# The seam between attention and the gate units: when the operand sums, the loads and the first unit's products run

## The chip, the cores and the metric

The kernel runs on one core of a Trainium2 chip. Five engines work side by side, each on its own stream of instructions: TensorE (PE, matmuls into PSUM), VectorE (DVE), ScalarE (ACT), GpSimd (POOL) and SyncE (SP), which here only issues transfers between the core's memory SBUF and the device memory. An engine takes its instructions in order: one that waits holds up all behind it. The metric is the device time of one execution in microseconds (us), lower is better.

## The reference

One layer of a streaming encoder on x, 1024 tokens by 1024 features, in fp32:

```python
h = rmsnorm(x, norm_mix_g[li])
z = h @ w_in[li]
qa, fa, ia, ga, qb, kb, vb, gate_a, gate_b = jnp.split(z, split_at, axis=-1)
oa = hgrn2_mixer(qa, fa, ia, ga, lower_bounds[li], hgrn_onorm_g[li])
ob = band_attention(qb, kb, vb, attn_qnorm_g[li], attn_knorm_g[li], attn_rel_bias[li])
merged = (jax.nn.sigmoid(gate_a) * (oa @ w_branch_a[li])
          + jax.nn.sigmoid(gate_b) * (ob @ w_branch_b[li]))
x = x + merged @ w_out[li]
...
```

A feed-forward block and an embedding block follow, which the change does not touch. What matters here are gate_a and gate_b: 2048 output features, 16 columns of 128, each a product of the normalized x with a block of `w_in`, then a sigmoid.

## The kernel before

**Numbers.** Every fp32 matrix is split in two parts: `hi`, a rounded copy in the matmul's type that ACT casts, and `lo`, the remainder that DVE or POOL subtracts. A product is three matmuls (hi·hi, hi·lo, lo·hi) for each 128 x 128 block against 512 tokens. `self.u` holds the eight feature blocks of x, scaled and split: eight pairs of tiles of 128 x 1024, the halves `h0` and `h1` being 512 tokens each.

**Gate columns.** The first four of the 16 columns are plain products (`PLAIN = 4`): per column two token halves of eight blocks, 24 matmuls each. Columns 0 and 1 are computed by `gate`, which attention draws on as filler between its own steps; columns 2 and 3 in `gate_units`. The other twelve columns go through six *units* of Strassen's scheme in Winograd's form (`strassen`), two columns by two token halves each: seven products of 12 matmuls instead of eight. Its seven activation operands are listed in `self.sops`: 0, 4 and 6 are plain blocks of u (odd features h1, even features h1, even features h0); 1, 2 and 3 are sums of blocks (`t32`, `t1`); 5 is a further sum that is written over the odd features' h0 of u, by `mix_last`, when no plain product needs that any more. The weight operands of a unit come from `strassen_weights`: sums of quarters of a raw weight pair that `strassen_load` brings, each split in hi (ACT) and lo (DVE or POOL).

**The sums.** `mix_sums` takes four pairs k of feature blocks from x again: it loads two tiles, scales the odd one on ACT, makes the sums on DVE in place, casts on ACT, subtracts on DVE. Four steps a pair, with a `yield` between them, so that `gate_units` can deal them out between the pieces of its plain products.

**Order.** PE's matmuls, and all operations called through `self.V`, `self.A` and `self.G`, run on their engines in the order of the program text (`Pinned`); so do all transfers on SP's queue (`load` and `store`). Operations called through `self.nc` are placed by the compiler's scheduler; POOL's sums of other weights (`quad_slow`), which the units carry along, are of that kind. A tile's buffer comes free after the last use of the tile; `self.slot()` takes one of 32 buffers of 128 x 1024, `self.stmp()` one of eight of 128 x 512, and a load waits on SP's queue until its buffer is free.

**The seam.** `attention` runs 34 turns (`whole = 32`, and two more to end the pipeline); in each it draws two pieces from `feed`, and after the last turn it gives out what is left of `feed`, the second half of column 1. Then `gate_units` starts `mix_sums` (line 774), loads the first unit's raw weights, applies the sigmoids of columns 0 and 1, and computes columns 2 and 3 while the sums and the first unit's weights are made on the other engines; in the first piece the outputs of two attention heads and columns 0 and 1 are stored (lines 793 to 795). Lines 801 to 806 end the sums and write the last operand, line 814 loads the second unit's weights. Line 832 runs the units; while a unit's products run, its `side` makes the next unit's weights.

In `strassen` (line 1405) three banks of PSUM are used, with products 3, 4, 5 and 6 added on top of a bank that DVE or ACT has read before:

```python
product(1, b2, True)
u2 = add(tmp(), p1, b2)
...
product(3, b2, False)
```

Product 3 may start only when the add in front of it has read b2.

Of the kernel before, what the change touches and what calls it, by code (L numbers as in the profile page):

```python
# [17 lines left out]
P = 128  # L18
# [23 lines left out]
def f32(ap):  # L42
    return ap.bitcast(F32)
# [13 lines left out]
class Trunk:  # L57
# [581 lines left out]
    def attention(self):  # L639

        steps = [(2 * two + p, b) for two in range(2) for b in range(8) for p in range(2)]
        whole = len(steps)
        feed = chain(self.feed, self.gate(self.gates, ahead=3), self.gate(self.gates, ahead=2))
        sc, pts = {}, {}

        def stack(n):
            if n >= whole:
                return iter(())
            p, b = steps[n]
            if b == 0:  # L650
                for h in range(2):
                    bt = self.small(640, tag="bias")
                    self.load(bt, self.d["bias"][2 * p + h])
                    self.bias[p, h] = bt
            return self.attn_stack(p, b)

        def scores(n, h):
            stages = self.attn_scores(*steps[n], h)
            sc[n, h] = (*next(stages), stages)

        def stage(n, h):
            if 0 <= n < whole:
                next(sc[n, h][2], None)

        def pt(n, h):
            if 0 <= n < whole:
                pts[n, h] = self.attn_pt(*sc[n, h][:2])

        def pv(n):
            if 0 <= n < whole:  # L670
                self.attn_pv(*steps[n], (pts.pop((n, 0)), pts.pop((n, 1))), sc[n, 0][1])

        for i in range(FIRST, 8):
            next(feed, None)
            if i == FIRST:
                self.hgrn_gate()
            if i == 7:
                drain(stack(0))
                drain(self.hgrn_out())
        for n in range(whole + 2):  # L680
            stage(n - 1, 1)
            next(feed, None)
            if n < whole:
                if steps[n][1] == 0:
                    self.ob.append(self.slot())
                scores(n, 0)
# [12 lines left out]
            if n == 0:  # L699
                self.keep_heads(self.oa, self.od, self.done_heads)  # L700
            if n == whole // 2 + 3:
                self.keep_heads(self.ob, self.obd, [0, 1])
            yield 0
        yield from feed


    def gate(self, keep, ahead=AHEAD):
# [6 lines left out]
            self.nc.vector.tensor_tensor(t[:, hs], ps, self.rb[:, hs], ALU.mult)  # L714
            yield 1296

    def mix_sums(self):

        V, A = self.V, self.A
        h0, h1 = slice(0, HALF), slice(HALF, T)  # L720
        g = lambda c: self.cols[:, C_MIX + c:C_MIX + c + 1]
        self.t32, self.t1 = [], []
        xs = []

        def load(k):
            xs.append((self.slot(), self.slot() if k < 2 else self.fp.tile([P, D], F32, tag="raw", name=f"xo{k}")))
            for j in range(2):
                self.load(xs[k][j], self.d["x"][2 * k + j])

        load(0)  # L730
        load(1)
        for k in range(4):
            xe, xo = xs[k]
            A.activation(xo, xo, AF.Copy, scale=g(2 * k + 1))
            yield
            V.scalar_tensor_tensor(xo[:, h0], xe[:, h0], g(2 * k), xo[:, h0], ALU.mult, ALU.subtract)
            V.tensor_tensor(xo[:, h1], xo[:, h0], xo[:, h1], ALU.add)
            V.scalar_tensor_tensor(xe[:, h0], xe[:, h0], g(2 * k), xo[:, h1], ALU.mult, ALU.subtract)
            V.scalar_tensor_tensor(xe[:, h1], xe[:, h1], g(2 * k), xo[:, h1], ALU.mult, ALU.subtract)
            yield  # L740
            hi, lo = self.slot(F32R), self.slot(F32R)
            self.t32.append((hi, lo))
            A.copy(hi, xo)
            if k % 2 == 0:
                self.t1.append((self.slot(F32R), self.slot(F32R)))
            hi1, lo1 = [t[:, k % 2 * HALF:k % 2 * HALF + HALF] for t in self.t1[-1]]
            A.copy(hi1, xe[:, h0])
            yield
            V.tensor_tensor(lo, xo, f32(hi[:, :]), ALU.subtract)
            V.tensor_tensor(lo1, xe[:, h0], f32(hi1), ALU.subtract)  # L750
            if k < 2:
                load(k + 2)
            yield
        self.mix_last = [(self.u[2 * k + 1][0][:, h0], self.u[2 * k + 1][1][:, h0], xs[k][0][:, h1]) for k in range(4)]

    def gate_done(self, c, half, ps):
        hs = slice(half * HALF, half * HALF + HALF)
# [10 lines left out]
    def gate_units(self, sums):  # L768
# [2 lines left out]
        h0, h1 = slice(0, HALF), slice(HALF, T)  # L771
        self.gd = [self.spill() for _ in range(2 * KC)]
        self.kept = []
        side = self.mix_sums()
        next(side)
        self.strassen_load()
        weights = self.strassen_weights()
        ts, self.gates = self.gates, []
        for c, t in enumerate(ts):
            A.activation(t, t, AF.Sigmoid)  # L780
# [1 line left out]
        for c in range(2, PLAIN):  # L782
            (w,) = self.weights(1, ahead=PLAIN - 1 - c)
            for half in range(2):
                stream = self.feature(w, self.u, half, piece=2)
                while True:
                    try:
                        next(stream)
                    except StopIteration as e:
                        ps = e.value  # L790
                        break
                    next(side, None)
                    if c == 2 and half == 0 and self.kept:
                        self.keep_heads(self.ob, self.obd, [2, 3])
                        self.gate_keep()
                    next(side, None)
                    if c > 2 or half:
                        next(weights, None)
                self.gate_done(c, half, ps)
                next(side, None)  # L800
        drain(side)
        drain(weights)
        for hi, _, x in self.mix_last:
            A.copy(hi, x)
        for hi, lo, x in self.mix_last:
            V.tensor_tensor(lo, x, f32(hi), ALU.subtract)
        u, t = self.u, self.t32
        cut = lambda pair, h: [x[:, h] for x in pair]
        four = range(4)
# [1 line left out]
            [cut(u[2 * k + 1], h1) for k in four], [cut(t[k], h1) for k in four],  # L811
            [cut(self.t1[k // 2], slice(k % 2 * HALF, k % 2 * HALF + HALF)) for k in four], [cut(t[k], h0) for k in four],
            [cut(u[2 * k], h1) for k in four], [cut(u[2 * k + 1], h0) for k in four], [cut(u[2 * k], h0) for k in four]]
        self.strassen_load()
        units = (2 * KC - PLAIN) // 2
        for n in range(units):

            def side():
                more = self.strassen_weights() if n + 1 < units else self.branch_first()
                if n == 0:  # L820
                    yield
                    yield
                next(more, None)
                if n + 2 < units:
                    self.strassen_load()
                yield
                for _ in more:
                    if n + 1 < units:
                        next(sums, None)
                    yield  # L830

            self.strassen(lambda c, half, ps: self.gate_done(PLAIN + 2 * n + c, half, ps), side())
            yield 0
        self.gate_keep()

# [482 lines left out]

    def strassen_load(self):
        ap = self.sorder[self.snext]  # L1320
        pool = (self.rp, self.fp)[self.snext % 2]
        self.snext += 1
        raws = []
        for j in range(2):
            self.n += 1
            raw = pool.tile([P, D], F32, tag="raw", name=f"wr{self.n}")
            self.load(raw, ap[:, j * D:j * D + D])
            raws.append(raw)
        self.sraw.append(raws)
# [32 lines left out]
    def strassen_weights(self):  # L1362

        V, A, G = self.V, self.A, self.G
        r1, r2 = self.sraw.pop(0)
        h0, h1 = slice(0, HALF), slice(HALF, D)

# [37 lines left out]
    def strassen(self, done, side):  # L1405


        V = self.V
# [9 lines left out]
        def add(out, x, y):  # L1418
            V.tensor_tensor(out, y, x, ALU.add)
            return out  # L1420
# [2 lines left out]
        p1 = tmp()  # L1423
        self.A.copy(p1, b1)
        next(side, None)
        product(1, b2, True)
        u2 = add(tmp(), p1, b2)
        next(side, None)
        product(2, b3, True)
        next(side, None)  # L1430
        product(3, b2, False)
        u3 = add(tmp(), p1, b2)
        add(u3, u3, b3)
        done(1, 0, u3)
        next(side, None)
        product(4, b1, False)
        done(0, 1, b1)
        next(side, None)
        product(5, b2, False)
        done(1, 1, add(tmp(), p1, b2))  # L1440
        next(side, None)
        product(6, b3, False)
        done(0, 0, add(u2, u2, b3))
        drain(side)

    def keep_acts(self, k):
# [553 lines left out]
```

## Time and profile before

| | |
|---|---|
| Time, median of 3 runs (lowest to highest) | 1603.34 us (1603.18 to 1604.33) |
| Time of the profiled execution | 1603.3 us |
| Its span, first to last instruction | 1600.6 us |
| PE busy in the span | 1568.0 us (98%) |
| DVE, ACT, POOL busy | 1173.3, 643.7, 796.5 us |
| Mean granted clock of PE | 0.997 |
| Attention's last copy / unit 0's first product / unit 1's first product, from the span's start | 531.72 / 558.95 / 585.26 us |

How to read the lines: a row of the timeline has the start and the length in us, the engine, the line of the kernel (L54 and L83 are helpers that record every pinned operation), the operation, output<-inputs by the program's names, the shapes, and in brackets how long the engine stood idle before it and what ended that. `s` is a slot, `pm` a bank of PSUM, `xo` and `wr` raw tiles, `whi`/`wlo` a unit's weights, `q` a sum of weights, `t` a half tile of `stmp`, `m` a small tile, `d` device memory. PE's matmuls overlap, so a pair that is listed at 0.62 us is followed by the next group 0.46 us later.

### The profile page before, as it was taken

The page shows a single profiled execution, that of the slowest core. Times are in us where ns is not written, and L with a number is a line of the kernel's source. Part 1 is how long each engine was busy: PE and PEld are TensorE (multiplying, and loading weights), DVE is VectorE, ACT ScalarE, POOL GpSimd, SP SyncE. Part 2 cuts the span into 40 slices and gives each one's busy share as a digit, 9 for nine tenths or more (in the row PEclk, how much of TensorE's full clock was granted, in tenths as well). Part 3 has the DMA queues.
Part 4 walks back from the last instruction along what each step waited for, and adds up shares of the span by engine and source line. Part 5 has one row for each costly group of instructions (what it writes and reads, how often), then busy time and mean ns, then how long its engine had stood idle before and what let it go on. Part 6 is the DMA issues. An engine that isn't in the chain of part 4 may idle for free.

```text
span 1600.6 us, 21819 instructions
## 1 busy us (share of the span) xinstructions
PE 1568.0 (98%) x8224; PEld 1309.6 (82%) x8224; DVE 1173.3 (73%) x1759; ACT 643.7 (40%) x1085; POOL 796.5 (50%) x449
## 2 busy tenths in 40 slices
PE   8999999999999989999999999999999999999997
PEld 6998988878888868888888788888888888888886
DVE  5656665389898687545898988888888866764658
ACT  5321221177677433321376332222322233445553
POOL 3422221356653156324430777777777764644554
PEclk9999999999999999999999999999999999999999
DMA  5101000245762355375144433233333268885334
GB/s 190 53 28 46 35 28 27 99 153 188 227 217 107 112 204 187 140 295 220 66 145 171 159 105 99 99 99 99 102 110 103 84 251 320 306 282 193 125 133 157
DMA packets 81609, 230.52 MB, mean 144 GB/s; under 512 B 9184, under 2 KB 9952, under 8 KB 80992
## 3 DMA queue, kind: packets, MB, share of 16 engines
q1 hardware_dynamic: 81360, 229.12, 41.3%
q8 instruction: 64, 1.05, 0.3%
q14 instruction: 41, 0.34, 0.1%
q10 hardware_dynamic: 144, 0.02, 0.0%
HBM read 163.82 MB, written 65.27 MB: 143 GB/s over the span
## 4 chain that ended last, share of the span: by engine, by line
PE 81%; DVE 9%; POOL 2%; ACT 1%; issue 1%; DMA 1%; SPq 0%; POOLq 0%; DVEq 0%; ACTq 0%
PE pm L83 79%; DVE s L54 4%; DVE m L54 3%; PE pm L86 2%; DVE q L54 1%; POOL m L556 1%; ACT s L54 0%; DVE pm L54 0%; DMA d<-s 0%; DVE t L54 0%; ACT m L54 0%; DMA s<-in_oq 0%; POOL wl L126 0%; DVE wlo L54 0%; DMA wr<-in_fm 0%
## 5 line engine op out<-in xcount | busy, mean ns | idle before, releaser
L83 PE MATMUL pm<-s,wh 128*128 128x512 f32 (+1 forms) x1712 | 532.1, 392 | 5.6 <-ACT wh L123 5.4
L83 PE MATMUL pm<-s,whi 128*128 128x512 f32 x1568 | 489.6, 393 | 7.1 <-DVE t L54 7.0
L126 POOL TENSOR_TENSOR wl<-wr,wh 128x1024 fp32r<-128x1024 f32 (+2 forms) x108 | 269.7, 2502 | 389.8 <-ACT wh L123 386.5
L83 PEld LDWEIGHTS pm<-s,wh 128*128 128x128 f32 x1712 | 319.7, 189 | 72.9 <-ACT wh L123 5.9
L83 PEld LDWEIGHTS pm<-s,whi 128*128 128x128 f32 x1568 | 295.3, 189 | 74.0 <-DVE t L54 8.3
L83 PE MATMUL pm<-s,wl 128*128 128x512 f32 (+1 forms) x856 | 333.8, 390 | 0.5 <-POOL wl L126 0.5
L54 DVE TENSOR_TENSOR s<-s,s 128x512 f32<-128x512 f32 (+4 forms) x213 | 257.5, 1237 | 92.7 <-ACT s L54 55.2
L83 PE MATMUL pm<-s,wlo 128*128 128x512 f32 x784 | 308.3, 393 | 0.4 <-POOL wlo L54 0.4
L83 PE MATMUL pm<-wh,s 128*128 128x256 f32 (+1 forms) x896 | 238.2, 340 | 0.0
L123 ACT CAST wh<-wr 128x1024 fp32r<-128x1024 f32 (+2 forms) x114 | 115.0, 1009 | 263.8 <-PE pm L83 139.2
L83 PEld LDWEIGHTS pm<-s,wl 128*128 128x128 f32 x856 | 161.2, 188 | 34.7 <-POOL wl L126 1.5
L83 PEld LDWEIGHTS pm<-s,wlo 128*128 128x128 f32 x784 | 147.7, 188 | 34.5 <-POOL wlo L54 0.8
L83 PEld LDWEIGHTS pm<-wh,s 128*128 128x128 f32 x896 | 154.6, 190 | 13.9 <-DVE s L341 0.2
L54 DVE TENSOR_TENSOR t<-pm,t 128x512 f32<-128x512 f32 x136 | 93.4, 687 | 83.1 <-PE pm L83 79.8
L54 DVE TENSOR_TENSOR s<-pm,s 128x512 f32<-128x512 f32 (+1 forms) x134 | 87.4, 681 | 84.2 <-PE pm L83 83.9
L83 PE MATMUL pm<-wl,s 128*128 128x256 f32 (+1 forms) x448 | 147.5, 329 | 0.8 <-POOL wl L126 0.8
L54 POOL TENSOR_TENSOR wlo<-wr,whi 128x512 fp32r<-128x512 f32 (+1 forms) x55 | 111.2, 2030 | 64.5 <-DMA xo<-in_x 48.6
L54 ACT CAST whi<-q 128x512 fp32r<-128x512 f32 (+1 forms) x81 | 61.4, 758 | 157.2 <-DVE q L54 134.9
L54 POOL TENSOR_TENSOR s<-s,t 128x512 f32<-128x512 f32 x44 | 76.9, 1747 | 86.6 <-ACT t L54 86.6
L54 ACT CAST s<-s 128x1024 fp32r<-128x1024 f32 (+1 forms) x94 | 90.2, 980 | 67.4 <-DVE s L54 33.5
L54 POOL TENSOR_TENSOR wlo<-q,whi 128x512 fp32r<-128x512 f32 x54 | 90.5, 1676 | 53.0 <-ACT whi L54 39.2
L83 PEld LDWEIGHTS pm<-wl,s 128*128 128x128 f32 x448 | 85.4, 191 | 6.3 <-POOL wl L126 1.0
(148 smaller groups left out, 1953.0 us busy)
## 6 DMA issues: line engine op xcount, KB each, us to landing
d<-s SPq DMA_DIRECT2D x147, 256.0 KB, 3.4
s<-d SPq DMA_DIRECT2D x67, 512.0 KB, 6.0
wr<-d SPq DMA_DIRECT2D x36, 512.0 KB, 3.9
s<-in_wq SPq DMA_DIRECT2D x22, 512.0 KB, 6.1
wr<-in_sg SPq DMA_DIRECT2D x22, 512.0 KB, 4.1
wr<-in_su SPq DMA_DIRECT2D x22, 512.0 KB, 4.0
s<-in_x SPq DMA_DIRECT2D x21, 512.0 KB, 7.7
d<-s SPq DMA_DIRECT2D x18, 512.0 KB, 4.1
```

What stands on the lines that cost most here:

```text
L54: return lambda *a, **k: self.trunk.order(op(*a, **k), self.key)
L83: return self.order(self.nc.tensor.matmul(*a, **k))
L86: return self.order(self.nc.tensor.transpose(*a, **k))
L123: self.nc.scalar.copy(hi[:, c], raw[:, c])
L126: rest.tensor_tensor(lo[:, c], raw[:, c], f32(hi[:, c]), ALU.subtract)
L556: nc.gpsimd.tensor_tensor(ss, ss, self.mhalf[:, 0:8], ALU.pow)
```

## The change

Four things move.

1. *The sums of pairs 0 and 1 start in attention.* In turn 30 attention loads the first unit's raw weights and then the four tiles of pairs 0 and 1 (`mix_start`); in turns 32 and 33, between the pieces of `feed` that are left and after them it makes their sums, to the end.
2. *Loads ahead of stores.* `gate_units` begins with the loads of pairs 2 and 3 (their odd tiles now in two half tiles of `stmp` each) and of the second unit's raw weights; the stores follow as before.
3. *The first unit's weights come ahead of the sums of pairs 2 and 3*, and all their remainders are subtracted by DVE, none by POOL (`strassen_weights(V)`). The last operand is written during the last half of column 3 (`mix_last`, now a generator).
4. *Unit 0 runs its products in the order 0, 4, 6, 1, 2, 3, 5* (`early`), each of 4, 5 and 6 in a bank of its own, which DVE adds up: six banks instead of three, and two adds more. The other units are as before.

```diff
@@ attention @@
+            if n == whole - 2:
+                self.strassen_load()
+                self.mix_start()
+                tail = chain(self.mix_sums(0), self.mix_sums(1))
+            if n >= whole:
+                next(tail)
             yield 0
-        yield from feed
+        for x in feed:
+            next(tail, None)
+            yield x
+        drain(tail)
...
+    def mix_start(self):
+
+        self.t32, self.t1, self.xs = [], [], []
+        for k in range(2):
+            xe, xo = self.slot(), self.slot()
+            self.mix_load(k, xe, [xo[:, :HALF], xo[:, HALF:]], xo)
+
+    def mix_load(self, k, xe, xo, whole=None):
+        self.xs.append((xe, xo, whole))
+        self.load(xe, self.d["x"][2 * k])
+        if whole is not None:
+            self.load(whole, self.d["x"][2 * k + 1])
+        else:
+            for j in range(2):
+                self.load(xo[j], self.d["x"][2 * k + 1][:, j * HALF:j * HALF + HALF])
...
@@ mix_sums(self, k): one pair, the same operations in five steps @@
+        for x, _ in parts:
+            A.activation(x, x, AF.Copy, scale=g(2 * k + 1))
+        yield
+        V.scalar_tensor_tensor(x0, xe[:, h0], g(2 * k), x0, ALU.mult, ALU.subtract)
+        V.tensor_tensor(x1, x0, x1, ALU.add)
+        yield
+        for x, c in parts:
+            A.copy(hi[:, c], x)
+        V.scalar_tensor_tensor(xe[:, h0], xe[:, h0], g(2 * k), x1, ALU.mult, ALU.subtract)
+        V.scalar_tensor_tensor(xe[:, h1], xe[:, h1], g(2 * k), x1, ALU.mult, ALU.subtract)
+        yield
+        A.copy(hi1, xe[:, h0])
+        for x, c in parts:
+            V.tensor_tensor(lo[:, c], x, f32(hi[:, c]), ALU.subtract)
+        yield
+        V.tensor_tensor(lo1, xe[:, h0], f32(hi1), ALU.subtract)
+        yield
...
@@ gate_units @@
-        side = self.mix_sums()
-        next(side)
+        for k in (2, 3):
+            self.mix_load(k, self.slot(), [self.stmp(), self.stmp()])
         self.strassen_load()
-        weights = self.strassen_weights()
+        side = chain(self.strassen_weights(V), self.mix_sums(2), self.mix_sums(3))
...
+                if c == PLAIN - 1 and half:
+                    drain(side)
+                    side = self.mix_last()
...
-                    if c > 2 or half:
-                        next(weights, None)
...
-        drain(weights)
-        for hi, _, x in self.mix_last:
-            A.copy(hi, x)
-        for hi, lo, x in self.mix_last:
-            V.tensor_tensor(lo, x, f32(hi), ALU.subtract)
...
-        self.strassen_load()
...
-            self.strassen(lambda c, half, ps: self.gate_done(PLAIN + 2 * n + c, half, ps), side())
+            self.strassen(lambda c, half, ps: self.gate_done(PLAIN + 2 * n + c, half, ps), side(), early=n == 0)
...
@@ strassen_weights @@
-        V, A, G = self.V, self.A, self.G
+        V, A, G = self.V, self.A, engine or self.G
...
@@ strassen @@
+        if early:
+            b4, b5 = self.mm(), self.mm()
+            product(4, b4, True)
+            done(0, 1, add(tmp(), p1, b4))
+            next(side, None)
+            product(6, b5, True)
+            next(side, None)
         product(1, b2, True)
         u2 = add(tmp(), p1, b2)
+        if early:
+            add(u2, u2, b5)
         next(side, None)
         product(2, b3, True)
         next(side, None)
         product(3, b2, False)
         u3 = add(tmp(), p1, b2)
-        add(u3, u3, b3)
-        done(1, 0, u3)
+        done(1, 0, add(tmp() if early else u3, u3, b3))
         next(side, None)
-        product(4, b1, False)
-        done(0, 1, b1)
+        if early:
+            done(0, 0, add(u2, u2, b3))
+        else:
+            product(4, b1, False)
+            done(0, 1, b1)
+            next(side, None)
+        if early:
+            b6 = self.mm()
+            product(5, b6, True)
+            done(1, 1, add(u3, u3, b6))
+        else:
+            product(5, b2, False)
+            done(1, 1, add(tmp(), p1, b2))
         next(side, None)
-        product(5, b2, False)
-        done(1, 1, add(tmp(), p1, b2))
-        next(side, None)
-        product(6, b3, False)
-        done(0, 0, add(u2, u2, b3))
+        if not early:
+            product(6, b3, False)
+            done(0, 0, add(u2, u2, b3))
         drain(side)
```

More of the change, by code (lines that the diff above doesn't have):

```diff
@@ L715, in gate, with mix_sums @@
             yield 1296
-    def mix_sums(self):
+    def mix_start(self):
[11 more added lines that the diff above has]
+                self.load(xo[j], self.d["x"][2 * k + 1][:, j * HALF:j * HALF + HALF])
+    def mix_sums(self, k):
         V, A = self.V, self.A
@@ L721, in mix_sums @@
         g = lambda c: self.cols[:, C_MIX + c:C_MIX + c + 1]
[L722 to L731, printed above, removed]
-        for k in range(4):
[L733 to L753, printed above, removed]
@@ L754, in mix_sums @@
-        self.mix_last = [(self.u[2 * k + 1][0][:, h0], self.u[2 * k + 1][1][:, h0], xs[k][0][:, h1]) for k in range(4)]
+        xe, (x0, x1), xo = self.xs[k]
+        hi, lo = self.slot(F32R), self.slot(F32R)
+        self.t32.append((hi, lo))
+        if k % 2 == 0:
+            self.t1.append((self.slot(F32R), self.slot(F32R)))
+        hi1, lo1 = [t[:, k % 2 * HALF:k % 2 * HALF + HALF] for t in self.t1[-1]]
+        parts = [(xo, slice(0, T))] if xo is not None else [(x0, h0), (x1, h1)]
+        for x, _ in parts:
+            A.activation(x, x, AF.Copy, scale=g(2 * k + 1))
@@ L756, in gate_done, with mix_last @@
+        yield
+        V.tensor_tensor(lo1, xe[:, h0], f32(hi1), ALU.subtract)
+        yield
+    def mix_last(self):
+        h0, h1 = slice(0, HALF), slice(HALF, T)
+        for k in range(4):
+            self.A.copy(self.u[2 * k + 1][0][:, h0], self.xs[k][0][:, h1])
+        yield
+        for k in range(4):
+            hi, lo = self.u[2 * k + 1]
+            self.V.tensor_tensor(lo[:, h0], self.xs[k][0][:, h1], f32(hi[:, h0]), ALU.subtract)
+            if k % 2:
+                yield
     def gate_done(self, c, half, ps):
@@ L1320, in strassen_load @@
         ap = self.sorder[self.snext]
-        pool = (self.rp, self.fp)[self.snext % 2]
+        pool = self.fp if self.snext % 2 else self.rp
         self.snext += 1
@@ L1360, in unit_up, with strassen_weights @@
         self.V.tensor_tensor(self.gu[c][:, hs], ps, self.gu[c][:, hs], ALU.mult)
-    def strassen_weights(self):
-        V, A, G = self.V, self.A, self.G
+    def strassen_weights(self, engine=None):
+        V, A, G = self.V, self.A, engine or self.G
         r1, r2 = self.sraw.pop(0)
@@ L1403, in strassen_weights, with strassen @@
         self.sready = (a11, cut(s21, h0), cut(s21, h1), s3, cut(a12, h0), cut(a12, h1), s4)
-    def strassen(self, done, side):
+    def strassen(self, done, side, early=False):
         V = self.V
```

## The prediction

> **What bounds the kernel now.** I read the busy shares first, then the waits of TensorE by stage, then the stretch around the seam in windows and in order of time.
>
> ```profile
> PE 1568.0 (98%) x8224; PEld 1309.6 (82%) x8224; DVE 1173.3 (73%) x1759; ACT 643.7 (40%) x1085; POOL 796.5 (50%) x449
> ```
>
> PE is busy for 1568.0 of 1600.6 us, so no change that leaves the matmuls alone can win more than its 32.6 idle us and what the clock loses. The windows cut the seam at PE's own steps: unit 0 of the Strassen units, the hole in it, the stretch after the hole, unit 1 up to its own small hole, and the following 19.11 us, in which seven products run without a gap.
>
> ```profile
> 515.00:531.60 16.60, 16.60 (x133) 13.39 (x130) 7.80 (x25) 6.61 (x14) 0.00 (x0) 1.00 0.08 33
> 558.95:585.26 26.31, 21.30 (x85) 16.71 (x84) 18.78 (x24) 11.06 (x19) 8.41 (x6) 0.94 0.48 170
> 567.80:572.69 4.89, 0.00 (x1) 0.00 (x1) 3.23 (x5) 3.62 (x8) 1.27 (x1) 0.98 0.74 215
> 572.69:576.33 3.64, 3.64 (x10) 2.87 (x10) 1.47 (x2) 0.62 (x1) 1.28 (x1) 0.56 1.00 351
> 585.26:594.55 9.29, 8.42 (x38) 6.58 (x36) 8.99 (x7) 3.45 (x7) 9.21 (x6) 1.00 0.81 270
> 594.55:613.66 19.11, 19.11 (x83) 15.66 (x84) 15.13 (x15) 7.73 (x12) 16.05 (x11) 1.00 0.75 254
> ```
>
> (Columns: length, then busy us of PE, PE's weight loads, DVE, ACT, POOL; granted clock, DMA share, GB/s.) Unit 0 takes 26.31 us where seven undisturbed products take 19.11, or 2.73 each: 7.20 us are lost. 4.89 is the hole. After it the clock is 0.56 for 3.64 us, which loses 3.64 x 0.44 = 1.60. In PE's order of time:
>
> ```profile
> 563.81 1.01 PE L83 MATMUL pm<-s,whi 128*128 128x512 f32 x2
> ...
> 564.89 0.63 PE L83 MATMUL pm<-s,whi 128*128 128x512 f32 x2
> ...
> 572.69 1.22 PE L83 MATMUL pm<-s,whi 128*128 128x512 f32 x2 [4.89 <-DVE t L54]
> ...
> 594.55 0.72 PE L83 MATMUL pm<-s,whi 128*128 128x512 f32 x2 [0.87 <-DVE t L54]
> ```
>
> The hole is product 3 waiting for the add that frees bank b2 (tile t). A smaller one, 0.87, stands at product 3 of unit 1. The pair at 563.81 is 0.38 longer than the pair at 564.89. The chain shows what made the add late:
>
> ```profile
> 564.19 1.77 DVE s L54
> ...
> 568.87 0.52 ACT s L54
> ...
> 569.41 1.07 DVE s L54 x2
> ...
> 571.36 0.68 DVE s L54
> 572.03 0.61 DVE t L54
> ```
>
> In front of the add, in DVE's fixed order, stand the four remainders of the operand that is written last (569.41 to 572.03), and they wait for ACT's casts. DVE and ACT are behind; the sums' arithmetic starts only when attention has ended. DVE had room earlier: 7.80 busy of 16.60 us from 515.00 to 531.60.
>
> **The change part by part.** PE's 84 matmuls a unit stay: nothing is removed there.
>
> *Sums of pairs 0 and 1 begin in turns 32 and 33.* Durations on DVE and on the engines it meets:
>
> ```profile
> 527.55 0.48 ACT L54 COPY m<-pm 128x384 f32<-128x384 f32 x1 [0.26 <-PE pm L86]
> ...
> 531.72 0.27 ACT L54 COPY s<-pm 128x128 f32<-128x128 f32 x1 [3.69 <-PE pm L83]
> ...
> 531.88 1.16 ACT L54 ACTIVATE s<-s,cols 128x1024 f32<-128x1024 f32 x1
> ...
> 533.07 0.75 DVE L54 SCALAR_TENSOR_TENSOR s<-s,cols,s 128x512 f32<-128x512 f32 x1 [1.91 <-ACT s L54]
> ...
> 537.38 0.69 DVE L714 TENSOR_TENSOR s<-pm,rb 128x512 f32<-128x512 f32 x1 [3.56 <-PE pm L83]
> ...
> 538.71 1.41 DVE L54 SCALAR_TENSOR_TENSOR s<-s,cols,s 128x512 f32<-128x512 f32 x2
> ...
> 569.41 2.62 DVE L54 TENSOR_TENSOR s<-s,s 128x512 fp32r<-128x512 f32 x4 [1.65 <-ACT s L54]
> ```
>
> ```profile
> L54 DVE TENSOR_TENSOR wlo<-q,whi 128x1024 fp32r<-128x1024 f32 x1 | 1.2, 1215 | 0.0
> ```
>
> The scaling of pair 0 (1.16) goes behind ACT's copy at 527.55, so 528.0 to 529.2, in 3.69 us in which ACT waited; DVE starts at 529.2 instead of 533.07. A pair costs DVE 0.75 + 0.69 + 1.41 + 1.22 + 0.69 = 4.76. In the tail nothing of attention stands behind these but the copy at 531.72, on which no matmul of the gates depends. Cost on PE: nothing. Without that cover it would be the 1.16 of one scaling.
>
> *The first unit's weight remainders go from POOL to DVE, pairs 2 and 3 behind them.*
>
> ```profile
> 547.79 1.36 POOL L54 TENSOR_TENSOR wlo<-wr,whi 128x512 fp32r<-128x512 f32 x1 [48.58 <-DMA xo<-in_x]
> ...
> 548.03 1.67 DVE L54 TENSOR_TENSOR xo<-xo 128x512 f32<-128x512 f32 x1
> ...
> 555.69 2.77 POOL L54 TENSOR_TENSOR wlo<-wr,whi 128x1024 fp32r<-128x1024 f32 x1 [6.54 <-ACT whi L54]
> ...
> 556.25 3.43 DVE L54 SCALAR_TENSOR_TENSOR s<-s,cols,xo 128x512 f32<-128x512 f32 x2
> ```
>
> DVE gets 3 x 0.69 + 1.22 = 3.3 us more, but beside POOL's operations its own were stretched: 1.67 for 0.69, 3.43 for 1.41, 1.77 (at 564.19) for 0.69, together 4.1. So the move is about even; I count +3.3 and let the 4.1 go, since undisturbed durations are used throughout. [...]
>
> DVE's ledger up to unit 0: four pairs 19.0, weights 4 x 0.69 + 1.22 = 4.0, moved remainders 3.3, last operand 2.6, five gate products 3.4: 32.3 us, from 529.2 to 561.5 without a wait. Waits for ACT were 1.91 and 1.65 above; two to four of them make it 565 to 568. The pairs themselves end some 4 us before that (2.6 and two gate products come after them).
>
> *Unit 0's order becomes 0, 4, 6, 1, 2, 3, 5.* Products 4 and 6 use plain blocks. From 558.95 at 2.73 each, product 1 needs the sums at 567.14 instead of 561.68; product 3 needs b2 free at 572.60 instead of 567.14; product 5, the only reader of the last operand, starts at 575.33. Ahead of the add u2 DVE has one more add and multiply (1.4), so it reaches it at 566.4 to 569.4, and product 1 ends at 569.87: in time by 2 us or more. The two more adds of unit 0 (0.69 each) are that one and one behind u2 that frees nothing PE waits for. If the early start brought nothing at all, the order alone would do most: add end 572.64 + 1.4 + 3.3 - 4.1 = 573.2 against 572.60, a hole of 0.6.
>
> *SP's order.*
>
> ```profile
> 488.04 2.25 SPq L78 DMA_DIRECT2D s<-in_x  x4
> ...
> 492.50 7.07 SPq L78 DMA_DIRECT2D wr<-in_sz  x2
> ...
> 527.32 12.20 SPq L78 DMA_DIRECT2D d<-s  x4
> ...
> 540.04 0.72 SPq L78 DMA_DIRECT2D xo<-in_x  x1
> ...
> 568.27 1.83 SPq L78 DMA_DIRECT2D wr<-in_sz  x4
> ...
> 574.65 0.78 DVE L54 TENSOR_TENSOR q<-wr,wr 128x512 f32<-128x512 f32 x1 [2.01 <-DMA wr<-in_sz]
> ```
>
> ```profile
> s<-in_x SPq DMA_DIRECT2D x21, 512.0 KB, 7.7
> ```
>
> The first four x loads now come behind the sz pair: 499.6 to 501.9, landed by 509.6, used at 528.0. They need four of the 32 slots; in turn 30 27 are held (16 of u, 2 of v, 6 of the keys, 2 of ob, 1 gate). If none came free before attention's last copy at 531.72, they would land near 540, DVE's ledger would start 11 us later and the hole would be back at 6 to 10 us. The count excludes it, and so does 488.04: the same four loads found slots long before attention ended. The x loads of pairs 2 and 3 (six, four of them halves) and unit 1's sz pair pass the four stores of 527.32. Their tiles lie where attention's were, so between 531.6 and the end of the tail near 540: landed by 548 at the latest, needed near 548; each late us eats one of the 5 us that the pairs have before 567.14. The stores behind them still wait for ACT's sigmoids (about 541 with the tail ahead), as the ones before did. The 2.01 us wait at 574.65 goes.
>
> *Sum.* 4.89 + 1.60 + 0.38 = 6.87. The hole of 0.87 in unit 1 I leave standing. The profiled execution took 1603.3 (span 1600.6 and 2.7 around it), as the median of the runs, 1603.34. 1603.3 - 6.9 = **1596.4**.
>
> **What is late next: unit 1.**
>
> ```profile
> 580.51 1.29 POOL L1046 TENSOR_TENSOR s<-s,s 128x512 f32<-128x512 f32 x1 [5.63 <-DVE q L54]
> ...
> 587.08 2.85 POOL L54 TENSOR_TENSOR wlo<-wr,whi 128x1024 fp32r<-128x1024 f32 x1
> ...
> 587.59 2.89 DVE L54 TENSOR_TENSOR q<-wr,q 128x512 f32<-128x512 f32 x1
> ...
> 589.90 3.45 POOL L54 TENSOR_TENSOR wlo<-q,whi 128x512 fp32r<-128x512 f32 x2
> ```
>
> POOL's remainder for product 3 ends near 591.6; PE wanted it at 593.45 (585.26 + 3 x 2.73). Now PE wants it at 578.06 + 8.19 = 586.25. If POOL's quad sums, whose place is not written by hand, start as late as now, that is a wait of 5.4 and with a new clock loss 7.0; if unit 1's remainders go first, as their raw weights now lie there early, nothing. I take nothing, being nearest to the POOL time free before 580.51 (5.63 us).
>
> **The rivals.**
> - *Unit 1 takes part of it back* (POOL late, or DVE stretched beside it as at 587.59). 1 to 7 us; I price it by the middle, 3.4: **1599.8**. For: POOL is 9.21 of 9.29 busy there. Against: the unit's weights start without the 2.01 wait. [...]
> - *The early start brings nothing* (x late, or ACT holds the tail): the hole of 0.6 remains: **1597.0**.
> - *Slower: DVE stays the bound through units 0 and 1.* Then its 3.3 of remainders and 1.4 of adds only lengthen its queue: the add at 593.8 that ends the 0.87 hole comes 4.7 later, at 598.5, and product 3 of unit 1 with it: 1603.3 + 4.7 = **1608.0**. It needs DVE to have no idle time to fill and the stretching to stay; against it stand its 8.8 idle us before 531.60 and the waits of 3.56, 2.01, 1.91 and 1.65.
>
> **How the numbers follow.** Forecast 0.62, early start without use 0.10, unit 1 0.20, slower 0.08. Low end: the 0.87 and the unnamed 0.3 of unit 0 go too, 1595.2, with 0.5 for the measurement: 1594.7. High end: 1601.5, inside rival 1, which leaves out its upper third, the slower case and little else. About 0.2% or 3.2 us can be told from no change, so faster means below 1600.1: 0.62 + 0.10 + over half of 0.20, and 0.79 after a little for what I overlook; within 0.13; slower 0.08.
>
> **What would show it.** Right: unit 0 takes 19 to 20 us at clock 1.00, no PE idle at product 3, x loads issued near 500, the raw weights of unit 1 before the stores, DVE busier from 528 to 533. Wrong: PE waits on DVE s at product 1, on POOL wlo or DVE t in unit 1, or a clock below 1.00 before 600.

## The result, and the profile after

| | before | after |
| --- | --- | --- |
| median of the runs compared, us | 1603.84 (1603.18 to 1604.98, 4 runs) | **1595.4** (1594.02 to 1597.2, 4 runs) |
| ratio, with its 95% interval | | 0.9947 [0.993, 0.9965] |
| the profiled execution, time and span, us | 1603.3, 1600.6 | 1595.63, 1593.7 |

The change made the kernel 8.4 us faster; the forecast was 1596.4. The interval lies wholly below 1.

Busy time of each engine on the page of the kernel after:

```profile
PE 1566.2 (98%) x8224; PEld 1309.3 (82%) x8224; DVE 1171.8 (74%) x1767; ACT 643.7 (40%) x1089; POOL 783.6 (49%) x445
```

The work has not shrunk: PE has as many matmuls and 1.8 us less busy time (the 3.41 us at clock 0.50, from 572.46 to 575.87 before, are gone), and DVE has 1172 us as before, in eight more instructions. So the gain is in when things happen. The windows after are cut at attention's last turns, then unit 0 and unit 1, each from its first matmul to the next unit's first (columns as in the prediction's windows):

```profile
515.00:531.60 16.60, 16.60 (x135) 13.40 (x131) 9.59 (x28) 7.65 (x15) 0.00 (x0) 1.00 0.18 64
559.08:578.46 19.38, 19.38 (x85) 15.79 (x84) 12.50 (x18) 7.28 (x12) 7.19 (x5) 1.00 0.45 150
578.46:597.80 19.34, 19.34 (x86) 15.80 (x84) 15.94 (x17) 7.91 (x13) 17.69 (x11) 1.00 0.79 243
```

Unit 0 takes 19.38 us where it took 26.31, at clock 1.00, and PE is busy in all of it. Unit 1 has no hole either and takes 19.34 us, so a product takes 2.76 us there (19.34 / 7). In the first row DVE is busy 9.59 of 16.60 us instead of 7.80: that is the arithmetic of the sums that has moved into attention's last turns. The chain of waits, cut to this stretch, says the same in one line:

```profile
527.81 112.28 PE pm L83 x503
```

From 527.81 on, through the plain columns and the first Strassen units, the chain is PE itself for 112 us; nothing releases it. DVE's timeline shows how much room there now is:

```profile
529.25 0.75 DVE L54 SCALAR_TENSOR_TENSOR s<-s,cols,s 128x512 f32<-128x512 f32 x1 [0.91 <-ACT s L54]
...
558.34 0.69 DVE L54 TENSOR_TENSOR s<-s,s 128x512 fp32r<-128x512 f32 x1
...
560.84 2.50 DVE L54 TENSOR_TENSOR s<-s,s 128x512 fp32r<-128x512 f32 x4 [1.21 <-ACT s L54]
...
566.44 0.69 DVE L54 TENSOR_TENSOR q<-wr,wr 128x512 f32<-128x512 f32 x1
567.16 0.69 DVE L54 TENSOR_TENSOR q<-q,wr 128x512 f32<-128x512 f32 x1
570.38 1.42 DVE L54 TENSOR_TENSOR t<-pm,t 128x512 f32<-128x512 f32 x2 [2.53 <-PE pm L83]
...
584.53 0.68 DVE L54 TENSOR_TENSOR t<-pm,t 128x512 f32<-128x512 f32 x1
```

The last row of pair 3 is the one at 558.34, so the pairs end at 559.0, just when unit 0 starts. The add u2, which PE waited 4.89 us for before, is the first of the two at 570.38, and now DVE waits 2.53 us for PE there: the wait has changed sides. DVE was through with everything in front of it at 567.85. PE wants bank b2 with the first matmul of product 3, the 61st of the unit:

```profile
572.91 0.64 PE L83 MATMUL pm<-s,whi 128*128 128x512 f32 x2
```

An add of 0.7 begun at 567.85 would have ended at 568.55, so DVE has 572.91 - 568.55 = **4.4 us of room**. Unit 1's add u2 (584.53) ends at 585.2, 1.5 us ahead of its product 3, which starts at 586.73.

SP's queue, issue time and how long the issue took:

```profile
499.77 2.10 SPq L78 DMA_DIRECT2D s<-in_x  x4
...
527.15 0.33 SPq L78 DMA_DIRECT2D s<-in_x  x1
...
533.22 0.85 SPq L78 DMA_DIRECT2D wr<-in_sz  x2
534.17 7.47 SPq L78 DMA_DIRECT2D d<-s  x4
```

The four x loads of pairs 0 and 1 go out from 499.77 on, within 2.10 us. The fifth, the first of pair 2, waits 25.3 us for PE to be done with a tile and goes out at 527.15; nothing behind it minds. Unit 1's raw weights (533.22) are ahead of the stores.

### The profile page after: what moved, and what is told of

It is laid out like the page before. It is cut to its first block, busy times and chain, and to the rows that moved or that the text cites. A ratio compares the mean times of both kernels' runs of the same rounds, so it can differ in the third digit from the quotient of the medians.

```text
span 1593.7 us, 21834 instructions
## 1 busy us (share of the span) xinstructions
PE 1566.2 (98%) x8224; PEld 1309.3 (82%) x8224; DVE 1171.8 (74%) x1767; ACT 643.7 (40%) x1089; POOL 783.6 (49%) x445
## 3 DMA queue, kind: packets, MB, share of 16 engines
q8 instruction: 64, 1.05, 0.2%
## 4 chain that ended last, share of the span: by engine, by line
PE 80%; DVE 9%; POOL 2%; ACT 2%; issue 2%; DMA 1%; SPq 0%; POOLq 0%; ACTq 0%; DVEq 0%
PE pm L83 77%; DVE s L54 5%; PE pm L86 2%; DVE m L54 2%; ACT s L54 1%; POOL wl L126 1%; POOL m L556 1%; DVE q L54 0%; DVE wl L126 0%; ACT wh L123 0%; DVE pm L54 0%; DMA d<-s 0%; DMA s<-in_oq 0%; POOL s L1075 0%; DMA wr<-d 0%
## 5 line engine op out<-in xcount | busy, mean ns | idle before, releaser
L126 POOL TENSOR_TENSOR wl<-wr,wh 128x1024 fp32r<-128x1024 f32 (+2 forms) x108 | 265.0, 2460 | 395.9 <-ACT wh L123 392.6
L54 POOL TENSOR_TENSOR wlo<-wr,whi 128x512 fp32r<-128x512 f32 (+1 forms) x53 | 107.5, 2037 | 74.9 <-ACT whi L54 74.1
```

The source lines that it names most:

```text
L54: return lambda *a, **k: self.trunk.order(op(*a, **k), self.key)
L126: rest.tensor_tensor(lo[:, c], raw[:, c], f32(hi[:, c]), ALU.subtract)
```

## The experiments

The theory: DVE was too late for the first unit because the sums' arithmetic began only after attention, and beginning it in attention's last turns is what removes the hole. The rivals: the new product order alone does it; moving the loads ahead of the stores does it; or taking the weights' remainders off POOL does it. Eleven kernels ran in three groups, each group beside runs of the kernel before on the same chip (medians 1604.02, 1603.85 and 1603.62). The table puts PE's waits in units 0 and 1 in the profiled execution together with an estimate of what the clock lost after them (PE's busy time at a granted clock of 0.50, times 0.5), and beside it the difference of the medians.

| | PE's waits in units 0 and 1 | clock | sum | median against before, us |
| --- | --- | --- | --- | --- |
| before | 4.89 + 0.87 | 1.60 | 7.4 | |
| after, taken again | 0 | 0 | 0 | -7.6 |
| order of products as before | 0 | 0 | 0 | -9.3 |
| order of products alone | 3.65 + 0.63 + 0.55 | 1.43 | 6.3 | +0.4 |
| no early start | 3.01 + 1.06 | 1.60 | 5.7 | -2.1 |
| loads behind the stores | 0 | 0 | 0 | -10.9 |
| remainders left on POOL | 0 | 0 | 0 | -6.1 |
| 2.4 us more on DVE | 0.57 | 0 | 0.6 | -7.8 |
| 9.8 us more on DVE | 4.97 + 0.60 | 2.54 | 8.1 | +0.2 |
| early start alone | 0.23 + 3.81 + 0.43 | 1.71 | 6.2 | -1.6 |
| early start and weights first | 0 | 0 | 0 | -7.8 |
| early start and loads first | 0.51 | 0 | 0.5 | -7.0 |

Two groups stand apart: with no long hole 6 to 11 us are won, with one 0 to 2. Within the first group the medians differ by more than the seam does (single runs of one kernel lie 3 to 7.5 us apart), so nothing is ranked there.

**Order of the products as before** (the rest of the change kept):

```diff
-            self.strassen(..., side(), early=n == 0)
+            self.strassen(..., side(), early=False)
```

> Unit 0 keeps its old order 0 to 6; early start, loads and weights first stay. If the early start of the sums carries the gain, nothing is lost: pair 3's remainder ends at 559.0 and product 1 would want it at 561.8, the add u2 can run at 565.1 and product 3 wants its bank at 567.3, so no hole, 1595.4 within 1. If the new order carries it, PE waits 3 to 5 us on DVE in unit 0: 1598.5 to 1602.

1594.74 (1593.39 to 1597.87), ratio 0.9937 [0.9912, 0.9961], and no PE wait between 545 and 615. Unit 0 starts at 561.28 in this execution, and in the old order its product 3, which wants b2, at 569.55. DVE's timeline:

```profile
567.31 0.69 DVE L54 TENSOR_TENSOR t<-pm,t 128x512 f32<-128x512 f32 x1 [1.18 <-ACT t L54]
```

In the old order u2 is the add at 567.31 and ends at 568.0, 1.5 us ahead. So with the sums begun early the new order is only spare room.

**Order of the products alone** (the kernel before, with the changed function and `early` for its first unit):

```diff
-            self.strassen(..., side())
+            self.strassen(..., side(), early=n == 0)
```

> The kernel before with the new order of unit 0 alone. The prediction's reckoning (order alone does most) would leave a hole of 0.6 at product 3 and 1597.0. Against it: product 6 now comes third, at 564.4, and wants the weights s4, which POOL ended at 569.7 in the kernel before: a hole of 5.3 there, with the clock's loss 5 to 7, so 1601 to 1604, nothing won.

1604.43 (1602.12 to 1605.19), ratio 0.9998 [0.9988, 1.0007]: nothing won. PE and ACT in order of time:

```profile
568.43 0.72 PE L83 MATMUL pm<-s,whi 128*128 128x512 f32 x2 [3.65 <-ACT whi L54]
...
569.78 0.80 PE L83 MATMUL pm<-s,wlo 128*128 128x512 f32 x1 [0.63 <-POOL wlo L54]
```

```profile
567.24 0.63 ACT L54 ACTIVATE t<-t 128x512 f32<-128x512 f32 x1 [3.14 <-DVE t L54]
567.77 0.60 ACT L54 CAST whi<-q 128x512 fp32r<-128x512 f32 x1
```

The hole moves to the third product, number 6, whose weight sum comes last in the kernel before. Its cast (567.77) stands on ACT behind a sigmoid that waits 3.14 us for DVE. DVE's lateness reaches PE by another way; reordering PE's demands does not help while the supply is late.

**No early start** (the change without beginning pairs 0 and 1 in turns 32 and 33; their x is still loaded in turn 30, weights first on DVE, loads first, new order):

```diff
-                tail = chain(self.mix_sums(0), self.mix_sums(1))
-            if n >= whole:
-                next(tail)
...
-        side = chain(self.strassen_weights(V), self.mix_sums(2), self.mix_sums(3))
+        side = chain(self.strassen_weights(V), *map(self.mix_sums, range(4)))
```

> The changed kernel without the early start: x of pairs 0 and 1 is still loaded in turn 30, but their sums are made in the gate units, behind the first unit's weights. By the prediction's reckoning a hole of 0.6, 1597.0. By the ledger as the trace of the changed kernel has it, DVE comes to the add u2 some 8 us later than 567.9: a hole of 3 to 4.5 at product 3, 1599 to 1601.

1601.88 (1599.82 to 1605.27), ratio 0.9989 [0.9978, 1.0]. PE's rows with a wait, then DVE's timeline:

```profile
578.95 1.22 PE L83 MATMUL pm<-s,whi 128*128 128x512 f32 x2 [3.01 <-DVE t L54]
...
595.53 0.72 PE L83 MATMUL pm<-s,whi 128*128 128x512 f32 x2 [1.06 <-DVE t L54]
```

```profile
575.54 0.69 DVE L54 TENSOR_TENSOR t<-pm,t 128x512 f32<-128x512 f32 x1 [1.17 <-ACT t L54]
...
576.88 0.68 DVE L54 TENSOR_TENSOR q<-wr,wr 128x512 f32<-128x512 f32 x1
577.60 0.69 DVE L54 TENSOR_TENSOR q<-q,wr 128x512 f32<-128x512 f32 x1
578.21 1.41 DVE L54 TENSOR_TENSOR t<-pm,t 128x512 f32<-128x512 f32 x2
```

The hole is back at product 3, behind u2 (578.21), and with it most of the loss: without the early start the other parts of the change win 2.1 us by the medians, and by the interval between nothing and 3.5. Just ahead of u2 stand unit 1's first two weight sums (576.88 and 577.60, 1.4 us) and a wait of 1.17 for ACT, which the prediction's 0.6 for this case had not counted.

**Loads behind the stores** (the change with the x loads of pairs 2 and 3 after the four stores, and unit 1's raw weights after column 3):

```diff
-        for k in (2, 3):
-            self.mix_load(k, self.slot(), [self.stmp(), self.stmp()])
-        self.strassen_load()
...
                         self.gate_keep()
+                        for k in (2, 3):
+                            self.mix_load(k, self.slot(), [self.stmp(), self.stmp()])
...
+        self.strassen_load()
         units = (2 * KC - PLAIN) // 2
```

> The changed kernel with the loads behind the stores again (pairs 2 and 3 behind the heads' stores, unit 1's raw weights behind column 3). If the loads' place matters, unit 1's raw weights land near 571, DVE waits 4 to 5 us for them at 566.4 in front of u2, and PE waits 1 to 2.5 us at product 3: 1596.5 to 1598. If it does not matter: no hole, 1595.4 within 1.

1593.11 (1592.78 to 1596.49), ratio 0.9934 [0.9912, 0.9956], no PE wait: the expected hole is not there. SP's queue in this kernel, then in the kernel before:

```profile
528.95 14.19 SPq L78 DMA_DIRECT2D d<-s  x4
...
549.39 12.75 SPq L78 DMA_DIRECT2D d<-t  x3
562.19 0.92 SPq L78 DMA_DIRECT2D wr<-in_sz  x2
```

```profile
546.10 22.07 SPq L78 DMA_DIRECT2D d<-t  x3
```

In the same place of the queue the raw weights now go out at 562.19, not at 568.27, since the three stores ahead of them take 12.75 us and not 22.07: they wait for gate products that DVE and ACT deliver. DVE waits 0.49 us for them here, where it waited 2.01. So the late weights of the kernel before were in the main a consequence of DVE's lateness, not a cause beside it.

**Remainders left on POOL:**

```diff
-        side = chain(self.strassen_weights(V), ...
+        side = chain(self.strassen_weights(), ...
```

> The changed kernel with the first unit's weight remainders on POOL again. DVE loses 3.3 us of work and gets some 4 us of stretching beside POOL: it comes to u2 within 1.5 us of 567.9, no hole, 1595.4 within 1. If POOL's slower remainders decide (s4 wanted third), PE waits at product 4 or 6 on POOL wlo: 1597 to 1600.

1597.75 (1595.45 to 1600.18), ratio 0.9957 [0.9942, 0.9971], no PE wait. DVE, then POOL:

```profile
544.24 2.88 DVE L54 TENSOR_TENSOR q<-wr,q 128x512 f32<-128x512 f32 x1
...
568.20 0.69 DVE L54 TENSOR_TENSOR q<-q,wr 128x512 f32<-128x512 f32 x1
```

```profile
543.83 2.74 POOL L54 TENSOR_TENSOR wlo<-wr,whi 128x1024 fp32r<-128x1024 f32 x1 [0.59 <-ACT whi L54]
```

DVE has four instructions fewer and is no earlier: it is through with the work ahead of u2 at 568.89, 9.8 us after unit 0's start at 559.12, where the change has 8.8 (567.85 after 559.08). Most of the 3.3 us that POOL takes off it comes back: a 0.69 us sum is stretched to 2.88 beside POOL's 2.74 us subtraction, and two more operations beside POOL by 0.3 and 0.5.

**More work on DVE** (two, and in a second kernel eight, extra 1024-wide subtractions at the end of pair 1, which write the same values again):

```diff
         V.tensor_tensor(lo1, xe[:, h0], f32(hi1), ALU.subtract)
+        if k == 1:
+            for _ in range(8):
+                V.tensor_tensor(lo, xo, f32(hi[:, :]), ALU.subtract)
```

> Two more subtractions of 128x1024 (1.22 us each) in DVE's tail, 2.4 us, results unchanged. The slack at product 3 is 4 us (DVE at the add by 567.9, its end wanted at 572.6): no hole, 1595.4 within 1. If DVE's place in the seam has no slack, 2.4 more: 1597.8.

> Eight more of them, 9.8 us. By the ledger the sums of pair 3 end 1.5 us after product 1 wants them and u2 ends 4.1 us after product 3 wants its bank: 5 to 6.5 us of holes, with the clock's loss up to 8: 1600.5 to 1603.5. If DVE is not what the seam hangs on: 1595.4 within 1.

With two: 1596.01 (1594.75 to 1598.55), ratio 0.9948 [0.9931, 0.9965]. With eight: 1604.05 (1602.43 to 1609.48), ratio 1.0007 [0.9995, 1.002]. DVE with two more, then DVE and PE with eight more:

```profile
572.21 1.42 DVE L54 TENSOR_TENSOR t<-pm,t 128x512 f32<-128x512 f32 x2 [0.56 <-PE pm L83]
```

```profile
577.82 1.41 DVE L54 TENSOR_TENSOR t<-pm,t 128x512 f32<-128x512 f32 x2
```

```profile
578.56 1.22 PE L83 MATMUL pm<-s,whi 128*128 128x512 f32 x2 [4.97 <-DVE t L54]
...
595.55 0.72 PE L83 MATMUL pm<-s,whi 128*128 128x512 f32 x2 [0.60 <-DVE t L54]
```

2.4 us more only shorten DVE's wait for PE, from 2.53 to 0.56. 9.8 us more bring back the whole loss. DVE begins u2 (577.82) 18.2 us after unit 0's start at 559.61, where the change had the way clear after 8.8: 9.4 us later. Less the 4.4 us of room that makes 5.0, and the hole is 4.97. So the room is as large as it was read, and DVE's queue ahead of u2 decides. The wait of 0.60 stands in unit 1 and is not part of this sum.

**Early start alone** (the kernel before with pairs 0 and 1 begun in attention's last turns; weights and remainders in their old places and on POOL, stores first, old order), and **early start with the loads of pairs 2 and 3 ahead of the stores**. The first, against the kernel "loads behind the stores" with `early=False`:

```diff
-        side = chain(self.strassen_weights(V), self.mix_sums(2), self.mix_sums(3))
+        side = chain([None], self.mix_sums(2), self.mix_sums(3))
+        weights = self.strassen_weights()
...
-                if c == PLAIN - 1 and half:
-                    drain(side)
-                    side = self.mix_last()
...
                     next(side, None)
+                    if c > 2 or half:
+                        next(weights, None)
...
+        drain(weights)
+        drain(self.mix_last())
```

The second differs from the first by this:

```diff
+        for k in (2, 3):
+            self.mix_load(k, self.slot(), [self.stmp(), self.stmp()])
         side = chain([None], self.mix_sums(2), self.mix_sums(3))
...
                         self.gate_keep()
-                        for k in (2, 3):
-                            self.mix_load(k, self.slot(), [self.stmp(), self.stmp()])
```

> The kernel before with the early start of pairs 0 and 1 alone: the first unit's weights are made late and on POOL, unit 0 in its old order, x of pairs 2 and 3 behind the four stores. If the early start alone carries the gain, pair 2 follows at 540 instead of 547 and the add u2 comes at 565, in time: 1595.4 within 1.5. If the early start needs something to fill the wait for x: the stores leave near 541 to 543, x of pair 2 lands near 550, DVE stands idle from 540 till then and ends no earlier than before: a hole of 4 to 7 in unit 0, 1602 to 1606.

> As the one with the early start alone, but x of pairs 2 and 3 loaded ahead of the stores, as in the changed kernel. x lands by 541, so DVE goes on at 540: no hole in unit 0, 1595 to 1597. If the weights' place is what counts, the hole stays: 1600 or more.

Alone: 1602.04 (1598.4 to 1605.33), ratio 0.9989 [0.998, 0.9998]. With the loads: 1596.61 (1594.8 to 1598.41), ratio 0.9954 [0.9942, 0.9967]. Of the first, SP's queue, DVE and PE:

```profile
542.83 0.40 SPq L78 DMA_DIRECT2D s<-in_x  x1
```

```profile
550.12 0.75 DVE L54 SCALAR_TENSOR_TENSOR t<-s,cols,t 128x512 f32<-128x512 f32 x1 [8.93 <-ACT t L54]
...
564.58 3.36 DVE L54 TENSOR_TENSOR wlo<-q,whi 128x1024 fp32r<-128x1024 f32 x1
```

```profile
568.00 0.50 PE L83 MATMUL pm<-s,wlo 128*128 128x512 f32 x1 [3.81 <-DVE wlo L54]
```

DVE begins early and then stands for 8.93 us: the x of pair 2 is issued only at 542.83, behind the stores, and ACT scales it ahead of DVE. The work that slips, here a weight remainder of 3.36 us (1.22 at 559.60 in the kernel before), makes PE wait 3.81. Of the second, DVE:

```profile
542.15 0.75 DVE L54 SCALAR_TENSOR_TENSOR t<-s,cols,t 128x512 f32<-128x512 f32 x1 [1.85 <-ACT t L54]
...
566.73 0.68 DVE L54 TENSOR_TENSOR t<-pm,t 128x512 f32<-128x512 f32 x1
```

The wait is 1.85, and u2 (566.73) ends at 567.41, where PE starts product 3 at 567.54, without a wait. It is in time by 0.1 us. The first unit's remainders are still on POOL here, so that alone makes no hole either.

**Early start with the first unit's weights first on DVE** (stores first, old order; the kernel "loads behind the stores" with `early=False`):

```diff
-            self.strassen(..., side(), early=n == 0)
+            self.strassen(..., side(), early=False)
```

> Early start and the first unit's weights first on DVE, and nothing else: stores ahead of loads, unit 0 in its old order. The weights fill DVE while x of pairs 2 and 3 comes (till near 549). u2 comes within 1 us of when product 3 wants its bank (567 after a start of unit 0 at 559): no hole or one below 1, 1595 to 1597. If two of the parts together are needed: a hole of 2 or more, 1598 to 1602.

1595.82 (1593.34 to 1597.85), ratio 0.9946 [0.9932, 0.9959], no PE wait. DVE:

```profile
542.03 0.68 DVE L54 TENSOR_TENSOR q<-wr,wr 128x512 f32<-128x512 f32 x1
...
550.44 0.69 DVE L54 TENSOR_TENSOR wlo<-q,whi 128x512 fp32r<-128x512 f32 x1 [1.21 <-ACT whi L54]
551.06 0.75 DVE L54 SCALAR_TENSOR_TENSOR t<-s,cols,t 128x512 f32<-128x512 f32 x1
```

The x is as late as with the early start alone, but the weights fill DVE's time from 542.03 to 551.06, and nothing is left of the 8.93 us. So the early start needs one of two things behind it: loads early, or other work to do until they land. (This kernel also differs from the one with the early start alone in that DVE makes the remainders and the last operand is written earlier; the place of the weights was not run by itself.)

**The change, taken again** with the last group:

> The changed kernel once more, on the chip of the three beside it, so that they can be compared: 1595.4 within 1.5, no hole in units 0 and 1.

1596.04 (1594.78 to 1597.87), ratio 0.9952 [0.9939, 0.9964], no PE wait.

No version beats the change by more than the scatter: seven of them have no hole in unit 0, and their medians lie from 1593.11 to 1597.75, with a mean of 1595.7. Five of the eleven medians lie outside the times that were expected: the order alone, no early start and 9.8 us more by 0.4 to 0.9 us above, the remainders on POOL by 1.4 above and the loads behind the stores by 1.3 below. In the last two PE has no wait that would explain it.

## Why the prediction was right

- **The bound and the sum.** Right. Unit 0 got back 26.31 - 19.38 = 6.93 us, and the hole, the clock and the pair make 6.87. The 0.3 that the sum left unnamed was not there: the prediction's 19.11 us for seven undisturbed products leaves out the last matmul, and from first matmul to first matmul they take 19.34 (unit 1 above). Unit 1, whose hole the sum left standing, took 20.46 us before (585.26 to 605.72) and takes 19.34 now, 1.12 less, so the seam won 8.0 where 6.87 was summed. The profiled spans differ by 6.9 and the medians by 8.4; the seven versions without a hole in unit 0 lie 8.1 below the mean of the three medians of before, 1603.8. So the seam accounts for the gain. The 1.1 us between 8.0 and the single spans' 6.9 lies outside the seam: in the profile after, PE is idle 0.24 us more from 0 to 100, 0.22 more from 300 to 500 and 0.49 more from 780 to 1010; why was not followed.
- **Early start.** Right. ACT's scaling stands where it was put, and DVE began at 529.25 (forecast 529.2):

```profile
528.06 1.16 ACT L54 ACTIVATE s<-s,cols 128x1024 f32<-128x1024 f32 x1
```

- **DVE's ledger.** Right at the place that counts, partly by luck. DVE was through at 567.85, within the forecast 566.4 to 569.4. Over that stretch:

```profile
529.25:567.85 38.60, 38.60 (x184) 31.60 (x183) 33.70 (x49) 23.20 (x35) 0.07 (x1) 1.00 0.47 162
```

  DVE was busy for 33.70 us, just what the ledger has (32.3 + 1.4), and idle for 4.9, within the 3.5 to 6.5 that it allowed. But the busy time agrees because two errors cancel: the ledger left out unit 1's two weight sums (566.44 and 567.16) and one of six gate products, 2.1 us together, and it added up listed lengths, which overlap where operations follow closely (those of this stretch add up to 35.6). The pairs ended at 559.0, 2 to 5 us ahead of the ledger's 561 to 564, since only 0.45, 0.41 and 1.21 us of the waits for ACT lie before their end.
- **Remainders to DVE: about even.** Right: with them left on POOL, DVE is 1.0 us later at the same place of the unit.
- **New product order.** It does what was said of it, but with the sums early it is not needed: the order as before has no hole either.
- **SP's order.** Slots were free for the four x loads, as the count of held tiles said; the fifth slot that the count leaves (27 of 32 held) was not, or the next load would not have waited until 527.15. That cost nothing. The loads ahead of the stores are one of two covers that suffice; with the weights first on DVE they are not needed.
- **Rival "early start brings nothing", 1597.0.** Its condition did not occur, and its price was wrong: with the early start taken out the time is 1601.88, since the hole is 3.01 and not 0.6, with the clock at 0.50 for 3.41 us, for which the price has nothing. The step that failed is "the order alone would do most"; the order alone won nothing (0.9998), because product 6 now comes third and its weight sum last, which the step had not looked at.
- **Rival "unit 1 takes part of it back", 1599.8.** Did not occur, but not for the reason given, that unit 1's remainders go ahead of POOL's quad sums. (Its 3.4 is also not the middle of 1 to 7, which is 4.0.) Only two of the four do, the second of them at 570.02:

```profile
570.02 2.41 POOL L54 TENSOR_TENSOR wlo<-wr,whi 128x1024 fp32r<-128x1024 f32 x1 [0.94 <-ACT whi L54]
574.83 1.29 POOL L1069 TENSOR_TENSOR s<-s,s 128x512 f32<-128x512 f32 x1 [2.40 <-DMA d<-t]
...
580.86 1.76 POOL L54 TENSOR_TENSOR wlo<-q,whi 128x512 fp32r<-128x512 f32 x1
```

  Product 3's remainder (580.86) still comes behind the four quad sums. What saves it is that these start at 574.83 and not at 580.51: it ends at 582.62, 4.1 us before PE starts product 3 at 586.73, and no PE wait stands there.
- **Slower: DVE stays the bound, 1608.0.** Did not occur; it takes some 4 us more on DVE before anything is lost. With 9.8 us more the time is that of the kernel before, so the mechanism was real and the room decided.

## What to carry to other kernels

When PE waits for the last item of another engine's fixed queue, ask where that engine was idle earlier and move its work there; here all the other parts together won 2 of 8 us without that. Work that is begun early also needs its next input early, or other work to fill the time until it lands: either was enough, neither had to be both. A late transfer may be a consequence of the late engine (its place in the queue is behind stores that wait for that engine), so look at what it stands behind before calling it a cause.

## What the runs showed of the hardware

The granted clock was 0.50 for 3.41 us in four kernels and for 6.83 us in a fifth, each time at a hole of 3.01 to 4.97 us in unit 0. Windows of the kernel without the early start: its hole, the 3.41 us before the half clock, and the stretch at half clock. Then of the kernel with eight more subtractions: its hole, and two stretches at half clock (columns as before, the granted clock third from the right):

```profile
575.94:578.95 3.01, 0.00 (x1) 0.01 (x1) 2.91 (x6) 1.71 (x3) 0.68 (x1) 0.96 0.88 208
575.33:578.74 3.41, 0.61 (x3) 0.18 (x1) 3.13 (x5) 1.68 (x4) 0.47 (x1) 1.00 0.72 169
578.74:582.15 3.41, 3.20 (x8) 2.54 (x9) 2.58 (x4) 1.63 (x2) 2.51 (x2) 0.50 0.98 363
```

```profile
573.59:578.56 4.97, 0.00 (x1) 0.01 (x1) 3.70 (x7) 2.81 (x5) 0.68 (x1) 0.82 0.55 129
576.80:580.21 3.41, 1.65 (x4) 1.37 (x5) 3.34 (x6) 2.99 (x4) 1.43 (x2) 0.50 0.84 237
580.21:583.63 3.42, 3.42 (x9) 2.65 (x9) 0.75 (x1) 0.00 (x0) 2.98 (x1) 0.50 0.99 378
```

At the hole of 3.01 us the clock was 0.50 for as long as at that of 4.89. At the waits of 0.23, 0.43, 0.55, 0.57, 0.60, 0.87 and 1.06 us it was 1.00; the 0.63 of the order alone lies inside that kernel's half-clock stretch. The half clock lasted 3.41 us in four kernels: before (572.46 to 575.87), no early start (578.74 to 582.15), order alone (569.23 to 572.65) and early start alone (568.84 to 572.25). With 9.8 us more on DVE it lasted 6.83 (576.80 to 583.63), twice that. It did not begin where the hole ended, but 0.2 us before that end in the first two, 0.8 us after it in the next two, and 1.8 us before it in the last. Two matmuls that are listed at 0.62 us at clock 1.00 were listed at 1.05 there (at 584.45 and 580.00 with 9.8 us more). Counted as half of PE's busy time in these stretches, an estimate, the loss is 1.4 to 1.7 us for 3.41 us and 2.54 for 6.83. By it these holes of 3 to 5 us cost 1.4 to 2.5 us more than their length, and the length alone doesn't say which (4.89 cost 1.6, 4.97 cost 2.54).

In the 3.41 us ahead of the half clock PE worked 0.00 us in the kernel before, 0.61 without the early start, 0.72 with the order alone, 0.84 with the early start alone and 0.20 with 9.8 us more on DVE. In the last it worked 1.65 in the first 3.41 us at half clock, and the clock was 0.50 for 3.42 us more. In the half-clock stretches after which the clock was 1.00 again PE worked 2.87 to 3.42 us. These are five cases, and they do not show what sets the clock. Nor do they show what a wait between 1.06 and 3.01 us does: in these two units no run had one.
